# SSM layer of a decoder trunk: a group's convolution in seven steps, decay rows loaded on ScalarE's queue, and a new order of the blocks

## The chip, the core and the metric

The kernel runs on one core of a Trainium2 chip. Its time is the device time of one execution in microseconds (us); the median of three runs is given where several were made. Engines: PE (TensorE, matmuls), DVE (VectorE), ACT (ScalarE), POOL (GpSimd) and SP (SyncE, which issues transfers).

## The reference

A trunk of two layers on 256 tokens of width 2048: an attention mixer (MLA) and a state-space mixer (SSM, Mamba-2), each followed by a squared-ReLU MLP. The change touches only the SSM mixer:

```python
def ssm_mixer(h, w_in, conv_w, conv_b, dt_bias, a_log, d_skip, norm_g, w_out):
    z, xbc, dt = jnp.split(h @ w_in, [SSM_D_INNER, SSM_D_INNER + SSM_CONV_DIM], axis=-1)
    xbc = jax.nn.silu(causal_depthwise_conv(xbc, conv_w, conv_b))        # 4 taps in time
    xs, b_in, c_in = jnp.split(xbc, ...)       # x: 8 groups of 8 heads of 64; B, C: 8 groups of 128
    dt = jax.nn.softplus(dt + dt_bias)
    y = ssd_chunked_scan(xs, dt, -jnp.exp(a_log), b_in, c_in)            # one chunk of 256
    y = (y + d_skip * xs) * jax.nn.silu(z)
    y = y * lax.rsqrt(mean(y * y over a group) + RMS_EPS) * norm_g
    return y @ w_out

# in the scan, per head: cum = cumsum(dt * a); decay = exp(cum[l] - cum[s]) for s <= l
#   y[l] = sum_s (C[l] . B[s]) * decay[l, s] * dt[s] * x[s]
```

## The kernel before

**Weights.** All weights stream from HBM in units of 128x1024 (512 KB). A unit is loaded on SP's queue into one of six `raw` buffers, ACT makes its high part `wh` (line 102), DVE its low part `wl` (line 103), with four buffers each, and PE multiplies both: a unit of an ordinary block is 12 matmuls of 512 columns (lines 339, 340, 343), a unit of the seven-product blocks six (lines 1158 to 1160; some of these units DVE makes first as sums of others, line 183). Conversion runs about three units ahead of PE.

**Ticks.** PE's instructions run in the order of the program. The other engines' orders are picked by the scheduler from what depends on what. The kernel places its small work with `later(n, fn)`: `fn` is written into the program n + 1 ticks on, where a tick ends two units of a block (`block`, or 5.4 us counted by `spend` in stage A). So a small matmul stands on PE at its tick, and everything behind it waits if its operand or its PSUM bank is not there.

**PSUM.** Four banks `acc`, two `yp`, two `sm`. `bank(False)` gives an `sm` bank, `bank(True)` alternates between `yp` and `sm`. A bank is taken again when its last reader is done.

**SSM, stage A.** Block B0 (projection of B for groups 0 to 3), the narrow block dt, then two passes `ssm_seven` of seven-product blocks with other units between them (SSM_FILLERS: C0 and x4, then x5 and x6; a filler accumulates in `yp`). A B or C block is evacuated (`evac`), and `conv` takes it in two halves: transposes to an `sm` bank (line 1216), ACT and three DVE taps per piece (lines 1222 and 1225), Tanh (1227) and the product (1228). dt's narrow result is folded (line 367), a chain of some 20 small DVE steps and ACT steps makes dt and log a (lines 1255 to 1271), `cums` multiplies by a triangle to get the running sums (1277) and writes them to HBM (`cumD`), `back` transposes them (1286).

**SSM, stage B.** SSM_ORDER lists the rest: v = the convolution of a group's x (`x_conv`), x7, B1, C1, z = a group's gate projection, o = output projection. `x_conv(g)` reads rows of x back from HBM (four shifted views, four tap weights and a bias), and DVE multiplies and adds over several ticks. With it goes `cb_group(g)` (lines 1302, 1303: the product of B and C into an `sm` bank, masked by DVE, copied by ACT at 1311). Then `ahead` puts eight heads on a queue and `across` computes the far half (line 1389). In each tick `pump` takes one or two heads: `head` loads the head's row of `cumD` to all partitions (`cm`, four buffers, line 1414, on SP's queue), ACT makes exponentials (lines 1419, 1421), DVE multiplies by cb (1426). After eight heads: the products (1437, 1438), POOL and DVE add up, and the group is `ready`. `z_block(g)` computes the gate's SiLU; `gate` runs when the group is ready: POOL product, ACT squares (line 296), reciprocal root, DVE product, a POOL-issued copy (`words`), and `transposes` to an `sm` bank (lines 322, 324), which ACT and DVE empty (299, 300).

Of the kernel before, what the change touches and what calls it, by code (L numbers as in the profile page):

```python
# [20 lines left out]
F32 = mybir.dt.float32  # L21
# [7 lines left out]
P = 128  # L29
S = 256  # L30
# [184 lines left out]
class Trunk:  # L215
    def __init__(self, tc, ctx, d, out):
        self.tc, self.nc, self.d, self.out = tc, tc.nc, d, out
        nc = self.nc
        pool = lambda name, bufs, **kw: ctx.enter_context(tc.tile_pool(name=name, bufs=bufs, **kw))
        self.c = pool("const", 1)  # L220
        self.st = pool("stat", 24)
        self.res = pool("res", 1)
        self.xtp = pool("xt", 8)
        self.k4 = pool("k4", 8)
        self.s2 = pool("s2", 7)
        self.gb = pool("gb", 2)
# [4 lines left out]
        self.queue, self.pump = [], None  # L231
        self.nsm = 0
        self.uid = 0
# [9 lines left out]
    def tick(self):  # L243
        ready = []
# [926 lines left out]
    def ssm_body(self, sp, dp, gain, later):  # L1171
# [14 lines left out]
        xg = [None] * GROUPS  # L1186
        hq, ready, gated, batch = [], set(), set(), []
        far = [None] * GROUPS
# [19 lines left out]

        def conv(ev, ct, dst, lag):

            def half(j):
                b = self.bank(False)
                for k in range(2):
# [15 lines left out]
            self.later(lag, lambda: half(0))  # L1229
            self.later(lag + 1, lambda: half(1))  # L1230

# [7 lines left out]

        def bc_block(name, i, accs=None):  # L1240
            if accs is None:
                accs = self.block([("si", name, i, q) for q in range(4)], xT)
            t = self.ktile(self.k4, F32)
            fm[name, i] = t
            conv(evac(accs), (32 if name == "B" else 40) + 4 * i,
                 lambda j: t[:, 2 * j:2 * j + 2].rearrange("p a b -> p (a b)"), 0)

        def dt_block():
            self.narrow_block(("si", "dt", 0, 0), self.xT, dt_chain)

        def dt_chain(b):
# [23 lines left out]
            def cums():  # L1275
                b = self.bank(False)
                nc.tensor.matmul(b[:64, 0:256], la[:, 0], tri, start=True, stop=False)
# [18 lines left out]

            self.later(2, cums)

# [30 lines left out]

        def x_conv(g):  # L1330
            xt = sp2.tile([P, 2, 512], F32, tag="xtm", name=f"xtm{g}", bufs=4)
# [10 lines left out]

            def fetch():
                with behind("last_load"):
                    nc.sync.dma_start(xt, x_rows(g, 0, 2))
                    weight(3)
                    load(2)
                    weight(2)
                    load(1)
                    weight(1)  # L1350
                    load(0)

# [6 lines left out]
            def mult():  # L1359
                with behind("last_lo"):  # L1360
                    nc.vector.tensor_tensor(xt, xt, both(3), ALU.mult)
                    tapped(2)
                with behind("last_load"):
                    weight(0)
                    weight(4)

# [10 lines left out]
            def ahead():  # L1377
                xg[g] = x
                dg = self.gain_tile(d["dsk"][g])
                for i in range(8):  # L1380
                    hq.append((g, i, dg))
                heads_of = lambda v: v.rearrange("p (h f) -> p h f", h=8)
# [9 lines left out]

                self.later(1, across)

            self.later(0, fetch)
            self.later(1, lambda: cb_group(g))
            self.later(2, mult)
            self.later(3, lambda: tapped(1))
            self.later(4, total)
            self.later(5, lambda: (silu(), ahead()))  # L1400

        def pump():
            for _ in range(2 if len(hq) > HEAD_BACKLOG else 1):
                if hq:
                    g, i, dg = hq.pop(0)
                    head(g, i, dg)
                    if i == 7:
                        break

        def head(g, i, dg):  # L1410

            h = 8 * g + i
            cm = sp2.tile([P, S], F32, tag="cm", name=f"cm{h}", bufs=4)
            nc.sync.dma_start(cm, cumD[h:h + 1].to_broadcast([P, S]))
            if i % 4 == 0:
# [13 lines left out]
            heads = batch[:]  # L1429
            batch.clear()  # L1430

            def products():
# [26 lines left out]
        def z_block(g):  # L1459
            accs = self.block([("si", "z", g, q) for q in range(4)], xT)  # L1460
            ng = self.gain_tile(d["sng"][g])
            ssq = self.stat(2)
# [31 lines left out]
        out = {}  # L1494

        def filler(tok):
# [4 lines left out]
            if o == 7:  # L1501
                x_block(i, out[0]) if kind == "x" else bc_block(kind, i, out[0])
            self.spend(2.72)

        with ExitStack() as first:
# [12 lines left out]
        for step in SSM_ORDER:  # L1518
# [5 lines left out]
            elif kind == "v":  # L1524
                x_conv(i)
            elif kind == "z":
# [4 lines left out]
            else:  # L1531
# [128 lines left out]
def sequence(d):  # L1660
# [40 lines left out]
    so = lambda k, nb: add(("so", k, nb), d["so"][k, nb])  # L1701
    si("B", 0)
    add(("si", "dt", 0, 0), d["sidt"], 16, 64)
    for p in range(2):
# [102 lines left out]
```

## Time and profile before

| what | value |
|---|---|
| three runs | 2347.49 us median (2343.76 to 2348.76) |
| profiled execution | 2347.11 us, its span 2345.2 us |
| granted TensorE clock, mean | 0.988 |
| instructions on PE / DVE / ACT / POOL | 10881 matmuls / 2257 / 2036 / 323 |
| moved by DMA | 569.74 MB, mean 243 GB/s |
| SSM in the profile | about 975 to 1560 us; stage B from 1172 us |

Durations and starts come from the profiled execution alone. A row of a timeline is start, duration, engine, line, operation, output and inputs, count, and in brackets the idle time before it with what ended it. A row of the waits is engine, output, line, what it waited for, then microseconds in total, times, and the longest. Rows of a stage table give the length, then the busy time of PE, PEld (weight load), DVE, ACT and POOL with instruction counts, the granted clock, the DMA engines' share and GB/s.

### The profile page before, as it was taken

The page shows a single profiled execution, that of the slowest core. Times are in us where ns is not written, and L with a number is a line of the kernel's source. Part 1 is how long each engine was busy: PE and PEld are TensorE (multiplying, and loading weights), DVE is VectorE, ACT ScalarE, POOL GpSimd, SP SyncE. Part 2 cuts the span into 40 slices and gives each one's busy share as a digit, 9 for nine tenths or more (in the row PEclk, how much of TensorE's full clock was granted, in tenths as well). Part 3 has the DMA queues.
Part 4 walks back from the last instruction along what each step waited for, and adds up shares of the span by engine and source line. Part 5 has one row for each costly group of instructions (what it writes and reads, how often), then busy time and mean ns, then how long its engine had stood idle before and what let it go on. Part 6 is the DMA issues. An engine that isn't in the chain of part 4 may idle for free. (4 is left out here: it accounts for less than half of the span.)

```text
span 2345.2 us, 30882 instructions
## 1 busy us (share of the span) xinstructions
PE 2292.8 (98%) x10881; PEld 1895.2 (81%) x10881; DVE 1968.5 (84%) x2257; ACT 1439.3 (61%) x2036; POOL 269.1 (11%) x323
## 2 busy tenths in 40 slices
PE   9999999999999999989999898999999999999999
PEld 7888888888888888767877677788888888888887
DVE  7776798899899887977869787985888899889985
ACT  7775566666656656556656565664566666666663
POOL 1530000000000000000002133231000000000000
PEclk9999999999999999989999999999999999999999
DMA  8545688888888877658797677876687888888875
GB/s 316 167 160 167 206 251 246 267 253 266 276 246 263 273 216 250 199 160 280 249 338 252 228 255 264 291 238 205 216 260 240 275 259 251 258 269 250 263 232 165
DMA packets 177050, 569.74 MB, mean 243 GB/s; under 512 B 20192, under 2 KB 29344, under 8 KB 176896
## 3 DMA queue, kind: packets, MB, share of 16 engines
q1 hardware_dynamic: 159328, 510.83, 65.5%
q0 software_dynamic: 15040, 52.68, 11.0%
q10 hardware_dynamic: 2528, 4.27, 0.5%
q8 instruction: 85, 1.39, 0.3%
q14 instruction: 69, 0.57, 0.1%
HBM read 542.23 MB, written 6.41 MB: 234 GB/s over the span
## 5 line engine op out<-in xcount | busy, mean ns | idle before, releaser
L102 ACT ACTIVATE wh<-wraw 128x1024 fp32r<-128x1024 f32 (+1 forms) x818 | 857.3, 1053 | 535.6 <-PE acc L340 197.6
L103 DVE TENSOR_TENSOR wl<-wraw,wh 128x1024 fp32r<-128x1024 f32 (+1 forms) x818 | 989.2, 1227 | 191.4 <-ACT wh L102 182.3
L617 PE MATMUL yp<-wh,k 128*128 128x512 f32 x896 | 349.3, 390 | 0.0
L619 PE MATMUL yp<-wh,k 128*128 128x512 f32 x896 | 348.8, 389 | 0.0
L618 PE MATMUL yp<-wl,k 128*128 128x512 f32 x896 | 348.6, 389 | 0.0
L102 ACT ACTIVATE wh<-wrx 128x1024 fp32r<-128x1024 f32 x192 | 203.3, 1059 | 177.0 <-PE yp L619 99.1
L103 DVE TENSOR_TENSOR wl<-wrx,wh 128x1024 fp32r<-128x1024 f32 x192 | 233.2, 1220 | 46.3 <-ACT wh L102 45.7
L339 PE MATMUL acc<-wh,k 128*128 128x512 f32 x496 | 197.0, 397 | 0.0
L619 PEld LDWEIGHTS yp<-wh,k 128*128 128x128 f32 x896 | 168.2, 188 | 35.0
L617 PEld LDWEIGHTS yp<-wh,k 128*128 128x128 f32 x896 | 168.2, 188 | 34.9
L618 PEld LDWEIGHTS yp<-wl,k 128*128 128x128 f32 x896 | 168.2, 188 | 34.9
L340 PE MATMUL acc<-wh,k 128*128 128x512 f32 x496 | 193.9, 391 | 0.0
L339 PE MATMUL acc<-wh,xt 128*128 128x512 f32 x448 | 181.6, 405 | 0.0
L340 PE MATMUL acc<-wh,xt 128*128 128x512 f32 x448 | 178.2, 398 | 0.3 <-DVE xt L482 0.2
L617 PE MATMUL st<-wh,xt 128*128 128x512 f32 x448 | 177.7, 397 | 0.0
L619 PE MATMUL st<-wh,xt 128*128 128x512 f32 x448 | 174.9, 390 | 0.0
L618 PE MATMUL st<-wl,xt 128*128 128x512 f32 x448 | 174.7, 390 | 0.0
L618 PE MATMUL st<-wl,sN 128*128 128x512 f32 x336 | 131.6, 392 | 2.0 <-DVE wl L103 2.0
L617 PE MATMUL st<-wh,sN 128*128 128x512 f32 x336 | 133.1, 396 | 0.0
L343 PE MATMUL acc<-wl,k 128*128 128x512 f32 x496 | 132.7, 389 | 0.0
L199 POOL DMA_DIRECT2D wrx<-mi x56 | 49.0, 876 | 723.8 <-DVE wl L103 513.7
L619 PE MATMUL st<-wh,sN 128*128 128x512 f32 x336 | 131.1, 390 | 0.0
(340 smaller groups left out, 3842.2 us busy)
## 6 DMA issues: line engine op xcount, KB each, us to landing
wraw<-mi SPq DMA_DIRECT2D x256, 512.0 KB, 5.7
wraw<-mo SPq DMA_DIRECT2D x256, 512.0 KB, 5.5
wraw<-si SPq DMA_DIRECT2D x160, 512.0 KB, 5.5
wraw<-so SPq DMA_DIRECT2D x64, 512.0 KB, 5.2
wrx<-mi SPq DMA_DIRECT2D x56, 512.0 KB, 5.3
wrx<-mi POOLq DMA_DIRECT2D x56, 512.0 KB, 7.6
wraw<-wo SPq DMA_DIRECT2D x32, 512.0 KB, 3.9
tap<-xD SPq DMA_DIRECT2D x24, 512.0 KB, 6.8
```

Source lines behind the costliest of these rows:

```text
L102: self.last = nc.scalar.activation(h[:, v], raw[:, v], AF.Copy)
L103: self.last_lo = nc.vector.tensor_tensor(lo[:, v], raw[:, v], h[:, v].bitcast(F32), ALU.subtract)
L199: nc.gpsimd.dma_start(st["b11"].tile, quarter(d, 1, 0), accum_op=ALU.add)
L339: nc.tensor.matmul(accs[t][:, :n], ah, wh[:, q, :], start=first and kt + q == 0, stop=False)
L340: nc.tensor.matmul(accs[t][:, :n], al, wh[:, q, :], start=False, stop=False)
L343: nc.tensor.matmul(accs[t][:, :n], lhs(kt + q, t)[0], wl[:, q, :], start=False, stop=en and q == nk - 1)
L617: nc.tensor.matmul(b, ah, wh, start=first and q == 0, stop=False)
L618: nc.tensor.matmul(b, ah, wl, start=False, stop=False)
L619: nc.tensor.matmul(b, al, wh, start=False, stop=last and q == 1)
```

## The change

B0 and C0 are ordinary blocks, both ahead of dt; C0 leaves the fillers. Their convolution halves are two ticks apart (C0's three, starting three ticks on), B's and C's in alternating `yp` and `sm` banks except C0's. The fold of dt comes six ticks after its block instead of one, `cums` four instead of two ticks after the fold's tick, `back` two ticks further. `x_conv` starts after a given number of ticks, splits its loads over two ticks, and puts cb_group, the multiplications, the total and the SiLU into five further ticks; `across` comes one tick later. The rows `cm` are loaded on ACT's queue, up to two heads ahead, and the heads go two to a tick always. A gate starts two ticks after the last addition, its transposes a tick later; the gain tiles are loaded at their use. SSM_ORDER is new. PE has the same instructions as before.

```diff
-        def conv(ev, ct, dst, lag):
+        def conv(ev, ct, dst, lag, gap, wide):
 
             def half(j):
-                b = self.bank(False)
+                b = self.bank(wide)
...
             self.later(lag, lambda: half(0))
-            self.later(lag + 1, lambda: half(1))
+            self.later(lag + gap, lambda: half(1))
...
-        def bc_block(name, i, accs=None):
+        def bc_block(name, i, lag=1, gap=2, wide=True):
...
-            self.narrow_block(("si", "dt", 0, 0), self.xT, dt_chain)
+            self.narrow_block(("si", "dt", 0, 0), self.xT, dt_chain, 6)
...
-                self.later(0, back)
+                self.later(2, back)
...
-            self.later(2, cums)
+            self.later(4, cums)
...
-        def x_conv(g):
+        def x_conv(g, wait):
...
-                self.later(1, across)
-
-            self.later(0, fetch)
-            self.later(1, lambda: cb_group(g))
-            self.later(2, mult)
-            self.later(3, lambda: tapped(1))
-            self.later(4, total)
-            self.later(5, lambda: (silu(), ahead()))
+                self.later(2, across)
+
+            self.later(wait, lambda: fetch(whole, lambda: weight(3), lambda: load(2), lambda: weight(2), lambda: load(1)))
+            self.later(wait + 1, lambda: fetch(lambda: weight(1), lambda: load(0)))
+            self.later(wait + 2, lambda: cb_group(g))
+            self.later(wait + 3, mult)
+            self.later(wait + 4, lambda: tapped(1))
+            self.later(wait + 5, total)
+            self.later(wait + 6, lambda: (silu(), ahead()))
 
         def pump():
-            for _ in range(2 if len(hq) > HEAD_BACKLOG else 1):
-                if hq:
-                    g, i, dg = hq.pop(0)
-                    head(g, i, dg)
+            for _ in range(2):
+                if cms:
+                    g, i, cm = cms.pop(0)
+                    head(g, i, cm)
                     if i == 7:
                         break
-
-        def head(g, i, dg):
+            while hq and len(cms) < 2:
+                g, i = hq.pop(0)
+                cm = sp2.tile([P, S], F32, tag="cm", name=f"cm{8 * g + i}", bufs=4)
+                nc.scalar.dma_start(cm, cumD[8 * g + i:8 * g + i + 1].to_broadcast([P, S]))
+                cms.append((g, i, cm))
+
+        def head(g, i, cm):
 
             h = 8 * g + i
-            cm = sp2.tile([P, S], F32, tag="cm", name=f"cm{h}", bufs=4)
-            nc.sync.dma_start(cm, cumD[h:h + 1].to_broadcast([P, S]))
...
-                    ready.add(g)
+                    ready[g] = self.ticks + 2
...
-                if g not in ready:
+                if self.ticks < ready.get(g, self.ticks + 1):
                     self.later(0, gate)
                     return
+                ng = self.gain_tile(d["sng"][g])
...
-                    self.later(2, lambda t=t, w=w: self.transposes(w, yT[g][0], yT[g][1], t, False))
-                self.later(2, lambda: gated.add(g))
+                    self.later(3, lambda t=t, w=w: self.transposes(w, yT[g][0], yT[g][1], t, False))
+                self.later(3, lambda: gated.add(g))
...
             bc_block("B", 0)
+            bc_block("C", 0, 3, 3, False)
             dt_block()
...
-                x_conv(i)
+                x_conv(i, int(step[3:] or 0))
...
-SSM_FILLERS = [[("C", 0), ("x", 4)], [("x", 5), ("x", 6)]]
-SSM_ORDER = ["v0", "x7", "B1", "v1", "z0", "v2", "z1", "C1", "v3", "z2", "z3", "v4", "o0a", "v5", "o0b", "z4", "v6",
-             "o1a", "v7", "o1b", "z5", "z6", "o2a", "z7", "o2b", "o3"]
+SSM_FILLERS = [[("x", 4)], [("x", 5), ("x", 6)]]
+SSM_ORDER = ["v0", "x7", "v1+2", "B1", "C1", "v2", "z0", "v3+2", "z1", "z2", "v4", "z3", "v5+4", "o0a", "o0b", "v6+2", "z4",
+             "o1a", "v7", "o1b", "z5", "z6", "z7", "o2a", "o2b", "o3"]
```

Three places show what moves. In these rows `sm_739` or `wh432` are single buffers (the last number is the program's own), and brackets name the engines or DMA lanes that the instruction waits for.

PE in stage A, before: the second half of a convolution (line 1216), the fold of dt (367) and the first matmuls of a seven-product block. 24 block matmuls stand between the first half (`sm_734`) and this one, and 72 between the fold and the running sums (1277).

```order
L343 MATMUL yp_738_9105<-wl431_9028,xt_664_8481 128x512
L1216 MATMUL sm_739_9141<-ident_97,s2_730_9044 128x128 [waits DVE_49]
L1216 MATMUL sm_739_9141<-ident_97,s2_731_9046 128x128
...
L367 MATMUL sm_742_9158<-cst_96,s2_733_9085 128x64 [waits DVE_49,PE_49,Activation_49]
...
L1158 MATMUL st_744_9188<-wh432_9048,xt_664_8481 128x512
L1159 MATMUL st_744_9188<-wh432_9048,xt_665_8482 128x512
```

The same place after; the half before it is `sm_751`.

```order
L1160 MATMUL st_749_9340<-wl455_9497,sN5_719_8906 128x512
L1216 MATMUL sm_755_9552<-ident_97,s2_741_9227 128x128 [waits PE_49]
L1216 MATMUL sm_755_9552<-ident_97,s2_742_9229 128x128
...
L367 MATMUL sm_758_9569<-cst_96,s2_744_9270 128x64 [waits DVE_49,PE_49,Activation_49]
...
L1158 MATMUL st_750_9369<-wh456_9509,sN6_724_8955 128x512
L1159 MATMUL st_750_9369<-wh456_9509,sN6_725_8956 128x512
```

The half now waits for no DVE work on its bank, 72 block matmuls stand between the halves, and 120 between the fold and the running sums.

PE in stage B, before: the transposes of gate 0 (lines 322 and 324), a tile for each half of the tokens (`sm_836`, `sm_837`), with ordinary block matmuls around them.

```order
L343 MATMUL acc_833_11446<-wl553_11450,xt_677_8587 128x512
L322 MATMUL sm_836_11535<-ident_97,tr_823_11366 128x128 [waits DMASW6_49,PE_49]
L322 MATMUL sm_836_11535<-ident_97,tr_823_11366 128x128 x3
L322 MATMUL sm_837_11542<-ident_97,tr_824_11369 128x128 [waits DMASW7_49,PE_49]
L322 MATMUL sm_837_11542<-ident_97,tr_824_11369 128x128 x2
L324 MATMUL sm_837_11542<-ident_97,s2_810_11148 128x128 [waits DVE_49]
L339 MATMUL acc_832_11445<-wh554_11467,xt_690_8693 128x512 [waits Activation_49]
```

After, the same two tiles are `sm_846` and `sm_847`; `sm_845` is the product of B and C for group 3 (lines 1301 and 1302 there, 1302 and 1303 before).

```order
L343 MATMUL acc_844_11725<-wl559_11665,xt_664_8481 128x512
L1301 MATMUL sm_845_11762<-k4_740_9226,k4_729_9039 128x256 [waits PE_49]
L1302 MATMUL sm_845_11762<-k4_740_9226,k4_729_9039 128x128
L322 MATMUL sm_846_11768<-ident_97,tr_834_11515 128x128 [waits DMASW6_49]
L322 MATMUL sm_846_11768<-ident_97,tr_834_11515 128x128 x3
L322 MATMUL sm_847_11775<-ident_97,tr_835_11518 128x128 [waits DMASW7_49,DVE_49]
L322 MATMUL sm_847_11775<-ident_97,tr_835_11518 128x128 x2
L324 MATMUL sm_847_11775<-ident_97,s2_823_11454 128x128
```

Three tiles of two `sm` banks now stand in one tick, and the last of them waits for DVE's reading of an earlier one.

ACT in stage B, before: the heads 19 and 20 (both of group 2) (lines 1419 and 1421) between conversions (102) and a piece of a convolution (1222); their rows come from SP's queue.

```order
L1419 ACTIVATE mt16_11601<-cm19_11695,pcum_8830 128x128 x2
L1421 ACTIVATE mt16_11601<-mt16_11601,lndt_8832 128x128 x2
L102 ACTIVATE wh562_11731<-wraw562_11612 128x1024
L102 ACTIVATE wh563_11786<-wraw563_11630 128x1024
L1222 ACTIVATE s2_845_11752<-sm_844_11747,cst_96 128x256
L102 ACTIVATE wh564_11804<-wraw564_11711 128x1024
L1419 ACTIVATE mt20_11779<-cm20_11777,pcum_8830 128x128 x2
```

After, around the same head 20 (lines 1417 and 1419 there), with the row loads (1407) on ACT itself and the emptying of gate 0's transposes (299):

```order
L102 ACTIVATE wh562_11746<-wraw562_11662 128x1024
L1419 ACTIVATE mt16_11702<-mt16_11702,lndt_8832 128x128
L1407 DMA cm20_11794<-cumD_8833 128x256
L1407 DMA cm21_11796<-cumD_8833 128x256
L1407 DMA cm22_11855<-cumD_8833 128x256
L102 ACTIVATE wh563_11800<-wraw563_11680 128x1024
L1417 ACTIVATE mt20_11846<-cm20_11794,pcum_8830 128x128 x2
L1419 ACTIVATE mt20_11846<-mt20_11846,lndt_8832 128x128 x2
L299 ACTIVATE k4_824_11457<-sm_846_11768 128x4x128
```

The rows of heads 20 to 22 are asked for together, one conversion ahead of the first use, and the emptying of `sm_846` stands behind that use.

More of the change, by code (lines that the diff above doesn't have):

```diff
@@ L230, in __init__ @@
         self.yp = pool("yp", 2, space=PSUM)
-        self.queue, self.pump = [], None
+        self.queue, self.pump, self.ticks = [], None, 0
         self.nsm = 0
@@ L243, in tick @@
     def tick(self):
-        ready = []
+        self.ticks += 1
         for e in self.queue:
@@ L1186, in ssm_body @@
         xg = [None] * GROUPS
-        hq, ready, gated, batch = [], set(), set(), []
+        hq, cms, ready, gated, batch = [], [], {}, set(), []
         far = [None] * GROUPS
@@ L1238, in evac @@
             return ev
-        def bc_block(name, i, accs=None):
-            if accs is None:
-                accs = self.block([("si", name, i, q) for q in range(4)], xT)
+        def bc_block(name, i, lag=1, gap=2, wide=True):
+            accs = self.block([("si", name, i, q) for q in range(4)], xT)
             t = self.ktile(self.k4, F32)
@@ L1245, in bc_block @@
             conv(evac(accs), (32 if name == "B" else 40) + 4 * i,
-                 lambda j: t[:, 2 * j:2 * j + 2].rearrange("p a b -> p (a b)"), 0)
+                 lambda j: t[:, 2 * j:2 * j + 2].rearrange("p a b -> p (a b)"), lag, gap, wide)
         def dt_block():
-            self.narrow_block(("si", "dt", 0, 0), self.xT, dt_chain)
+            self.narrow_block(("si", "dt", 0, 0), self.xT, dt_chain, 6)
         def dt_chain(b):
@@ L1341, in load, with fetch, whole @@
                 nc.sync.dma_start(tap[k], x_rows(g, 0, 2, k))
-            def fetch():
+            def fetch(*todo):
                 with behind("last_load"):
[L1345 to L1351, printed above, removed]
+                    for fn in todo:
+                        fn()
+            def whole():
+                nc.sync.dma_start(xt, x_rows(g, 0, 2))
             both = lambda k: cw[k].unsqueeze(1).to_broadcast([P, 2, 512])
@@ L1362, in mult @@
                     tapped(2)
-                with behind("last_load"):
-                    weight(0)
-                    weight(4)
+                fetch(lambda: weight(0), lambda: weight(4))
             def total():
@@ L1501, in filler @@
             if o == 7:
-                x_block(i, out[0]) if kind == "x" else bc_block(kind, i, out[0])
+                x_block(i, out[0])
             self.spend(2.72)
@@ L1702, in sequence @@
     si("B", 0)
+    si("C", 0)
     add(("si", "dt", 0, 0), d["sidt"], 16, 64)
```

5 lines of the change are left out of this document (2 added, 3 removed).

## The prediction

> **What bounds the kernel now.** I read the page first (busy shares), then PE's busy time and granted clock by stage, then the waits of PE from 900 us on, and last the timelines at those waits. The page:
>
> ```profile
> span 2345.2 us, 30882 instructions
> PE 2292.8 (98%) x10881; PEld 1895.2 (81%) x10881; DVE 1968.5 (84%) x2257; ACT 1439.3 (61%) x2036; POOL 269.1 (11%) x323
> ```
>
> PE is the bound, 52 us of the span are not PE, and the change removes no matmul. So the question is which of PE's idle time goes. Lines are those of the kernel before. By stage (the end of MLP 1, SSM projections with B0, C0, dt and the seven-unit blocks = stage A, the ordered part of SSM = stage B, MLP 2):
>
> ```profile
> 940.00:975.00 35.00, 35.00 (x180) 29.74 (x180) 33.00 (x40) 20.77 (x28) 3.37 (x7) 1.00 0.75 246
> 975.00:1172.00 197.00, 180.20 (x761) 146.18 (x760) 156.76 (x177) 113.87 (x127) 7.07 (x8) 0.94 0.71 219
> 1172.00:1560.00 388.00, 360.99 (x1937) 293.47 (x1936) 319.49 (x353) 237.83 (x460) 95.98 (x62) 0.96 0.79 269
> 1560.00:1660.00 100.00, 100.00 (x516) 82.95 (x515) 66.75 (x73) 47.05 (x58) 14.31 (x14) 1.00 0.70 218
> ```
>
> The columns after the length are PE, PEld, DVE, ACT, POOL busy, then the granted clock. PE is idle 197.0 - 180.2 = 16.8 us in A and 388.0 - 361.0 = 27.0 in B, 43.8 together, and never in the stages beside them; only there is the clock below 1.00. Who ends those waits:
>
> ```profile
> PE sm L1302 <- DVE s L1225: 10.5, 2, 6.0
> PE sm L322 <- DMA tr<-s: 6.6, 4, 4.0
> PE sm L1277 <- DVE dt L1270: 6.3, 1, 6.3
> PE sm L367 <- DVE s L1225: 4.4, 1, 4.4
> PE sm L1216 <- DVE s L1225: 4.3, 1, 4.3
> PE sm L1389 <- POOL s L1385: 3.9, 1, 3.9
> PE acc L343 <- DVE wl L103: 3.1, 2, 2.0
> PE sm L322 <- ACT cb L1311: 2.9, 1, 2.9
> PE yp L339 <- ACT s L1321: 1.5, 2, 1.0
> PE sm L1216 <- ACT s L1236: 0.2, 1, 0.2
> ```
>
> In A: 6.3 + 4.4 + 4.3 + 1.5 + 0.2 = 16.7. In B: 10.5 + 6.6 + 3.9 + 3.1 + 2.9 = 27.0. Nearly all are the small matmuls (lines 322 to 1389) that wait for a chain, or for one of the two `sm` banks, at the place in PE's order where their tick puts them. What such a wait costs is more than its length:
>
> ```profile
> 1232.45 1.19 PE L1302 MATMUL sm<-k,k 128*128 128x256 f32 x2 [5.96 <-DVE s L1225]
> ...
> 1284.45 0.50 PE L322 MATMUL sm<-ident,tr 128*128 128x128 f32 x4 [1.25 <-DMA tr<-s]
> 1286.19 0.59 PE L322 MATMUL sm<-ident,tr 128*128 128x128 f32 x3 [1.24 <-DMA tr<-s]
> ...
> 1287.67 0.63 PE L339 MATMUL acc<-wh,xt 128*128 128x512 f32 x1
> 1288.09 0.63 PE L340 MATMUL acc<-wh,xt 128*128 128x512 f32 x1
> ...
> 1429.76 1.19 PE L343 MATMUL acc<-wl,xt 128*128 128x512 f32 x4 [2.01 <-DVE wl L103]
> ...
> 1432.21 0.40 PE L339 MATMUL acc<-wh,xt 128*128 128x512 f32 x1
> 1432.44 0.39 PE L340 MATMUL acc<-wh,xt 128*128 128x512 f32 x1
> ```
>
> ```profile
> 1226.49:1232.45 5.96, 0.00 (x1) 0.03 (x1) 5.63 (x8) 0.62 (x2) 0.00 (x0) 0.86 1.03 407
> 1232.45:1238.00 5.55, 5.55 (x15) 4.48 (x16) 3.39 (x7) 1.51 (x3) 0.00 (x0) 0.53 0.67 207
> ```
>
> Right after the two gaps of 1.25 and 1.24 us matmuls start 0.42 us apart; after the gap of 2.01 they start 0.23 apart, the full pace (24 of them, one tick, are 5.5 us). The stage rows give the price in sum: (1 - 0.94) x 197 = 11.8 us and (1 - 0.96) x 388 = 15.5, together 27.3, if all of the slow clock fell on matmuls. Some falls into the gaps, where it costs nothing: by the last two rows, the gap of 5.96 us and what follows it, 0.14 x 5.96 = 0.8 inside and 0.47 x 5.55 = 2.6 behind. By that share (0.76) the clock costs 20.7 us, 0.47 for each us of idle time. A microsecond of idle time removed is then worth 1.47 us (1.62 if none falls into the gaps), and all that can be had is 43.8 x 1.47 = 64 us.
>
> On this the Trainium skill ("TensorE: Matmul & The Clock Gate", section "HAM oscillation — how this bites in real kernels") says that gaps over about 3.4 us bring the half clock. The pair of 1.25 and 1.24 us disagrees. By that rule the short waits that I leave below (8.9 us) would cost no clock, and the time would come out 0.47 x 8.9 = 4 us lower than mine.
>
> **Stage A, part by part.** B0's and C0's projections go ahead of dt's, their convolution halves come two and three ticks apart, the fold of dt six ticks after its block, and the running sums (line 1277) 120 block matmuls behind the fold where they were 72. 120 x 0.227 = 27.2 us; the chain took 72 x 0.227 + 6.3 = 22.6, so the 6.3 goes with 4.6 to spare. The fold and the second half no longer follow a half 24 matmuls earlier that still holds an `sm` bank (72 now): 4.4 and 4.3 go, and 0.2. With C0 no longer a filler in `yp`, 1.5 goes too. What is late next is DVE, whose order after C0's second half now reads six taps (line 1225), two makings of a sum of weights (line 183), the product (line 1228), dt's first steps with the reciprocal, and only then the low part of unit 460:
>
> ```profile
> L103 DVE TENSOR_TENSOR wl<-wraw,wh 128x1024 fp32r<-128x1024 f32 x66 | 79.7, 1221 | 18.4 <-ACT wh L102 17.4 <-PE st L1159 0.7
> ...
> L1225 DVE SCALAR_TENSOR_TENSOR s<-sm,cst,s 128x255 f32<-128x255 f32 (+2 forms) x24 | 11.4, 476 | 0.3
> L183 DVE TENSOR_TENSOR wraw<-wraw,wraw 128x1024 f32<-128x1024 f32 x8 | 9.8, 1223 | 4.5 <-DMA wraw<-si 4.5
> ...
> L1228 DVE SCALAR_TENSOR_TENSOR k<-s,s 128x512 f32<-128x512 f32 x4 | 2.7, 687 | 0.0
> ...
> L1260 DVE RECIPROCAL dt<-dt 128x128 f32<-128x128 f32 x1 | 0.9, 943 | 0.0
> ```
>
> 6 x 0.48 + 2 x 1.22 + 0.69 + 0.94 + five small steps that I put at 0.3 (half of a tap's size, half to two thirds of its time) + 1.22 for the unit itself = 9.7, and, as an estimate, three taps' time (1.4) for the turns through ACT: 11.1 us, while PE has 32 matmuls (7.3 us) to do before it needs that unit. 3.8 are lost there, and I add 2 for the six units behind it, each with some of dt's small steps in front. **A keeps 6 us of idle time** (0 if the converted units in store cover it, 14 if a second burst follows).
>
> **Stage B.** The product of a group's B and C (line 1302) leaves the tick of a convolution half and comes two ticks after the loads: the 10.5 goes. The gate's transposes get four ticks instead of three from the gate, 5.5 us more against a longest wait of 4.0: the 6.6 goes. The far product (line 1389) gets one more tick against 3.9: it goes. The 2.9 was a transpose that wanted the bank of a cb tile; that comes back in another shape. In the tick of gate 0's transposes the order now has cb of group 3 in one `sm` bank, and both transposes have to share the other: the second waits until ACT (line 299) and DVE (line 300) have emptied the first. On ACT there stands ahead of that emptying a head of group 2, the first use of a row asked for one unit earlier. Such rows were:
>
> ```profile
> L1419 ACT ACTIVATE mt<-cm,pcum x128: 384/387/405, 1203.6 to 1543.1; 128x128 f32<-128x128 f32 x128
> L1414 SPq DMA_DIRECT2D cm<-cumD x64: 319/422/1513, 1196.3 to 1534.9; - x64
> ...
>   DMA cm<-cumD: 37.8, 17
> ...
> DMA to landing us min/median/max: 3.0/5.4/9.0
> ```
>
> ```profile
> L299 ACT ACTIVATE k<-sm 128x512 fp32r<-128x512 f32 x12 | 6.6, 586 | 4.8 <-PE sm L322 4.7
> ```
>
> ```profile
> L300 DVE TENSOR_TENSOR k<-sm,k 128x512 fp32r<-128x512 f32 x12 | 7.9, 683 | 0.3 <-ACT k L299 0.3
> ```
>
> The wait is 0.59 + 0.68 = 1.3 us if ACT stands ready, and 1.3 + 5.4 + a head's 1.2 = 7.9 if ACT has just issued the loads; I take the middle, 4.6. The same three tiles meet once more, at gate 1 with cb of group 4: again 4.6 (1.3 to 7.9). The far product of group 1 takes the bank of cb 2, whose last reader on ACT also stands behind a load: 1.8 (0 to 4.4). In group 0 the rows are asked for just ahead of each use, and the units converted behind them come late: 2 (0 to 8). The 3.1 for `wl` stays (0 to 8), since DVE's work is the same. **B keeps 4.6 + 4.6 + 1.8 + 2 + 3.1 = 16.1 us.**
>
> The moved loads themselves: 64 issues leave SP (0.42 us each there, 27 us that delay no weight as far as the waits show) and stand on ACT. With the heads two to a tick, ACT's share of a group is six ticks, 32.7 us. Its pace:
>
> ```profile
> 1203.56 0.70 ACT L1419 ACTIVATE mt<-cm,pcum 128x128 f32<-128x128 f32 x2 [2.04 <-DMA cm<-cumD]
> ...
> 1204.74 0.68 ACT L1419 ACTIVATE mt<-cm,pcum 128x128 f32<-128x128 f32 x2
> ...
> 1220.18 2.00 ACT L102 ACTIVATE wh<-wraw 128x1024 fp32r<-128x1024 f32 x2
> ```
>
> 12 conversions at 0.96, 8 heads at 1.18 and 8 issues at 0.42 are 24.3; of ACT's other work in B (237.8, less 115 conversions at 1.05 and 64 heads at 1.38 by their busy times, is 29) 3.6 falls to a group: 27.9, which leaves 4.8 us. There are four buffers of rows. The first four heads' rows are asked for well ahead; the fifth's goes out one conversion before its use, so ACT stands 5.4 - 1.0 = 4.4 us once per group: just within the 4.8, and no more than before (37.8 / 8 = 4.7 per group). So the move is taken at nothing beyond the terms above. The convolution's loads, weights and products are the same instructions in other ticks, on SP and DVE; SP ends none of PE's waits above, and the DVE work that moves is the cover that rival 2 takes away. The gain tiles, loaded a tick or more before use either way, are taken at nothing too; a late one would hold the gate's last step, which has the four ticks as cover.
>
> The Trainium skill ("DMA: Bandwidth & Descriptors", section "Issuing engines are not separate DMA queues") says that all issuers' transfers share the same 16 DMA engines and that another issuer saves issue time alone. By it the landing stays near 5.4, as taken. Were ACT's queue free of the weights in front, with the shortest landing of 3.0, each of the three waits above that stand behind a row would lose up to 2.4 us, some 11 us with the clock. No run shown so far decides it.
>
> **Sum.** Idle time left 6 + 16.1 = 22.1; gone 43.8 - 22.1 = 21.7; by 1.47 that is 31.9 us. The profiled execution took 2347.1 (span 2345.2 and 1.9 around it), the median of the runs is 2347.5, so the two serve alike: 2347.1 - 31.9 = 2315.2, or **2315**.
>
> **Rivals.**
> 1. *The waits are covered.* Converted units and ACT's slack swallow the new bank waits; some 5 us stay: 38.8 x 1.47 = 57, that is 2290. For it: each new wait has an end near zero. Against: two transposes share one bank by the order itself. Chance 0.16.
> 2. *DVE is next.* DVE is busy 157 of 197 us in A and 319 of 388 in B, and B would end nearer 360; the waits named go, but PE waits for `wl` in their place. If 37 of the 43.8 us stay, 6.8 x 1.47 = 10 us are gained: 2337. For it: the burst found in A. Against: only 3.1 us of the waits were for `wl`. Chance 0.14.
> 3. *The asking ahead is not ahead, and ACT becomes the bound (slower).* If not one but three and more of the four later rows of a group are exposed one after the other, ACT stands 13.2 us and more against 4.8 of slack: 8.4 x 8 = 67 us, about all that could be had, so three is the point from which the kernel gets slower. At 3.5 it is (15.4 - 4.8) x 8 = 85 us on a floor of 2347.1 - 64 = 2283: 2368. For it: ACT works in order, so that every conversion behind a row waits with it. Against: the four rows go out in two or three issues that stand together, and land together. Chance 0.10.
>
> **How the numbers follow.** My forecast has 0.60: 2315, by its own ends 2290 to 2340. About 0.2% (4.7 us) is what a measurement of this kernel can tell from no change. The range from 2288 to 2343 leaves out rival 3, half of rival 1 and a corner of rival 2, 0.2 together. Faster: 0.60 + 0.16 + 0.09 of rival 2 = 0.85; same 0.05; slower 0.10.
>
> **What would show it.** Right: in the waits of PE lines 1302, 1277, 367 and 1389 for DVE and POOL are gone or under 1 us; what stands there is line 322 and the block lines waiting for DVE or ACT, some 22 us in sum; the clock reads 0.97 or 0.98 in both stages; ACT's wait for the rows is 30 to 45 us. Wrong: PE waits for `wl` or `wh` by more than 15 us (rival 2), ACT's wait for the rows is above 100 us (rival 3), idle time in SSM under 8 us (rival 1), or the granted clock stays at 0.95 while the idle time falls, which would break the factor of 1.47.

## The result, and the profile after

The changed kernel takes 2331.91 us (median, 2330.64 to 2335.67) against 2347.51 for the kernel before in the same session: the ratio is 0.9939, 95% interval 0.9922 to 0.9956. It is faster by 15.6 us, half of the 32 that were forecast. Its profiled execution took 2331.0 us.

The page, then the two stages of SSM. The border between them is the first matmul of block x7, at 1169.39 us before and 1153.29 after, and stage B ends 16.0 us before the old end. First before:

```profile
975.00:1169.39 194.39, 177.59 (x749) 144.01 (x748) 155.09 (x176) 111.88 (x124) 7.07 (x8) 0.94 0.71 218
1169.39:1560.00 390.61, 363.60 (x1948) 295.64 (x1947) 321.17 (x355) 239.82 (x463) 95.98 (x62) 0.96 0.80 269
```

and after:

```profile
span 2329.2 us, 30832 instructions
PE 2281.0 (98%) x10881; PEld 1886.9 (81%) x10881; DVE 1971.9 (85%) x2257; ACT 1437.2 (62%) x2036; POOL 254.7 (11%) x323
```

```profile
975.00:1153.29 178.29, 169.79 (x762) 139.28 (x761) 153.50 (x177) 110.04 (x124) 7.07 (x8) 0.97 0.77 236
1153.29:1544.00 390.71, 358.35 (x1997) 290.84 (x1996) 320.87 (x352) 237.28 (x462) 82.22 (x62) 0.97 0.80 269
```

Stage A is 194.39 - 178.29 = 16.1 us shorter, which is the whole difference. Stage B is as long as it was. PE stands idle in it for 390.7 - 358.4 = 32.3 us where it was 27.0, and its busy time fell by as much as that grew (363.6 to 358.4), which goes with the clock of 0.97 for 0.96. The waits of PE after, in SSM (engine, output, line, what ended the wait; total, times, longest):

```profile
PE y L1437 <- DVE s L1225: 10.0, 1, 10.0
PE sm L322 <- DVE k L300: 9.5, 1, 9.5
PE sm L367 <- DVE s L1225: 8.1, 1, 8.1
PE acc L339 <- ACT wh L102: 4.7, 4, 1.7
PE acc L343 <- DVE wl L103: 4.5, 3, 2.9
PE sm L1301 <- DVE k L300: 3.0, 1, 3.0
PE sm L1216 <- ACT cb L1310: 0.6, 1, 0.6
PE st L1160 <- DVE wl L103: 0.4, 2, 0.2
```

The waits that the change was to end are gone: line 1302 (10.5), the gate's transposes for their copy (6.6), the far product (3.9), the running sums (6.3). New ones of the same size stand in stage B, three of them for a PSUM bank. The first, from PE's timeline:

```profile
1225.21 0.60 PE L1216 MATMUL yp<-ident,s 128*128 128x128 f32 x4
1231.21 0.34 PE L1437 MATMUL y<-xtm,mt 128*64 128x64 f32 x4
1241.50 3.34 PE L1437 MATMUL y<-xtm,mt 128*64 128x64 f32 x60 [9.96 <-DVE s L1225]
```

B1's second convolution half went into a `yp` bank at 1225.2, and group 0's products need both `yp` banks 6 us later. DVE gives the bank back only when the six taps of that half are done, and it was that late:

```profile
1234.54 0.48 DVE L1225 SCALAR_TENSOR_TENSOR s<-yp,cst,s 128x255 f32<-128x255 f32 x1
...
1239.85 1.50 DVE L1225 SCALAR_TENSOR_TENSOR s<-yp,cst,s 128x255 f32<-128x255 f32 x3
```

The second is the wait that the prediction named, the two transposes of gate 0 that share one `sm` bank. ACT (first fence) emptied its part 2.8 us after PE's start at 1293.75, DVE (second fence) only at 1303.0, behind all this:

```profile
1296.00 0.57 ACT L299 ACTIVATE k<-sm 128x512 fp32r<-128x512 f32 x1
```

```profile
1296.58 0.68 DVE L1424 TENSOR_TENSOR mt<-mt,cb 128x512 f32<-128x512 f32 x1
1297.18 1.21 DVE L103 TENSOR_TENSOR wl<-wraw,wh 128x1024 fp32r<-128x1024 f32 x1
1298.32 1.27 DVE L1449 SCALAR_TENSOR_TENSOR xtm<-xtm,y 128x512 f32<-128x512 f32 x2
1299.52 1.37 DVE L1424 TENSOR_TENSOR mt<-mt,cb 128x512 f32<-128x512 f32 x1
1300.81 0.48 DVE L1305 SCALAR_TENSOR_TENSOR cb<-sm,tri 128x128 f32<-128x128 f32 x2
1301.21 1.89 DVE L103 TENSOR_TENSOR wl<-wraw,wh 128x1024 fp32r<-128x1024 f32 x1
1303.02 0.68 DVE L300 TENSOR_TENSOR k<-sm,k 128x512 fp32r<-128x512 f32 x1
```

### The profile page after: what moved, and what is told of

Read it like the earlier page. It is cut to its first block, busy times and chain, and to the rows that moved or that the text cites. A ratio compares the mean times of both kernels' runs of the same rounds, so it can differ in the third digit from the quotient of the medians.

```text
span 2329.2 us, 30832 instructions
## 1 busy us (share of the span) xinstructions
PE 2281.0 (98%) x10881; PEld 1886.9 (81%) x10881; DVE 1971.9 (85%) x2257; ACT 1437.2 (62%) x2036; POOL 254.7 (11%) x323
## 4 chain that ended last, share of the span: by engine, by line
PE 88%; DVE 5%; DMA 4%; ACT 2%; issue 1%; POOL 0%; SPq 0%; ACTq 0%; DVEq 0%
PE yp L619 9%; PE yp L618 9%; PE yp L617 9%; PE acc L339 8%; PE acc L343 8%; PE acc L340 8%; PE st L618 7%; PE st L619 7%; PE st L617 7%; DMA cm<-cumD 2%; DVE wl L103 2%; PE st L1160 1%; PE st L1158 1%; PE st L1159 1%; PE yp L339 1%
## 5 line engine op out<-in xcount | busy, mean ns | idle before, releaser
L102 ACT ACTIVATE wh<-wraw 128x1024 fp32r<-128x1024 f32 (+1 forms) x818 | 856.1, 1052 | 522.4 <-PE acc L340 183.9
L103 DVE TENSOR_TENSOR wl<-wraw,wh 128x1024 fp32r<-128x1024 f32 (+1 forms) x818 | 999.3, 1240 | 197.9 <-ACT wh L102 186.4
L102 ACT ACTIVATE wh<-wrx 128x1024 fp32r<-128x1024 f32 x192 | 203.3, 1059 | 169.8 <-PE yp L619 102.9
L103 DVE TENSOR_TENSOR wl<-wrx,wh 128x1024 fp32r<-128x1024 f32 x192 | 233.7, 1222 | 40.7 <-ACT wh L102 40.2
L339 PE MATMUL acc<-wh,xt 128*128 128x512 f32 x480 | 193.0, 402 | 2.7 <-ACT wh L102 1.7
L340 PE MATMUL acc<-wh,xt 128*128 128x512 f32 x480 | 188.9, 394 | 0.0
L343 PE MATMUL acc<-wl,xt 128*128 128x512 f32 x480 | 129.4, 392 | 0.1
```

What stands on the lines that cost most here:

```text
L102: self.last = nc.scalar.activation(h[:, v], raw[:, v], AF.Copy)
L103: self.last_lo = nc.vector.tensor_tensor(lo[:, v], raw[:, v], h[:, v].bitcast(F32), ALU.subtract)
L339: nc.tensor.matmul(accs[t][:, :n], ah, wh[:, q, :], start=first and kt + q == 0, stop=False)
L340: nc.tensor.matmul(accs[t][:, :n], al, wh[:, q, :], start=False, stop=False)
L343: nc.tensor.matmul(accs[t][:, :n], lhs(kt + q, t)[0], wl[:, q, :], start=False, stop=en and q == nk - 1)
```

## The experiments

All times are medians of four runs or more; each ratio is to the kernel before, timed beside it. The changed kernel (2331.91, ratio 0.9939) was timed in a session of its own, so a difference to it in microseconds can be off by one or two: by the two ratios the 22.5 us of e5_sp below are 21.6 and the 15.3 of e12_ahead 14.1.

**Which stage gave the gain.** Two kernels, each with one stage's part.

> The kernel before with stage A's part alone: B0 and C0 as blocks ahead of dt with their new spacing, the fold six ticks on, the running sums and the step behind them later; the ordered stage B as before. Theory 1 (all of the gain comes from stage A; in stage B each wait removed was replaced by a bank wait of the same size): 16 us under before, 2331, waits in stage B as before (27 us). Rival (the two stages lean on each other, the new stage B gives some and the new stage A some): 2336 to 2342.

The main edits to the kernel before (lines are left out at the dots):

```diff
...
+            bc_block("B", 0, 1, 2, True)
+            bc_block("C", 0, 3, 3, False)
...
+            self.narrow_block(("si", "dt", 0, 0), self.xT, dt_chain, 6)
...
+                self.later(2, back)
...
+            self.later(4, cums)
...
+SSM_FILLERS = [[("x", 4)], [("x", 5), ("x", 6)]]
...
```

Measured: 2333.11, ratio 0.9947 (0.9935 to 0.9960), 12.2 us under the kernel before.

> The changed kernel with stage A's part undone: C0 a filler again, old lags there; all of the new stage B. Theory 1: no gain, 2345 to 2350, with stage A's 16.8 us of idle time back and some 32 us of idle time in stage B. Rival (stage B by itself gives what was forecast for it): 2332.

The main edits to the changed kernel (the old places of the fold, of `cums` and of `back` are among the lines left out):

```diff
...
-            bc_block("B", 0)
-            bc_block("C", 0, 3, 3, False)
+            bc_block("B", 0, 0, 1, False)
...
-SSM_FILLERS = [[("x", 4)], [("x", 5), ("x", 6)]]
+SSM_FILLERS = [[("C", 0), ("x", 4)], [("x", 5), ("x", 6)]]
...
```

Measured: 2346.87, ratio 1.0004 (0.9995 to 1.0013). Theory 1 held: the gain is stage A's (12 us of the whole change's 16, with intervals that overlap), and the new stage B by itself is worth nothing that can be measured.

**Are the new waits worth their length?** Three kernels take one each away.

> The changed kernel with both halves of B1's and C1's convolution in sm banks, so that no half holds a yp bank ahead of group 0's products. Theory 1 (the 10.0 us wait of the products is one for a bank): it goes, with the half clock behind it 10 to 14 us, 2318 to 2322, unless the halves then wait for each other in sm. Rival (DVE is full there, and PE would wait for DVE's next product anyway, as low parts of weights): at most 3 us, 2329 to 2333.

```diff
-                bc_block(kind, i)
+                bc_block(kind, i, 1, 2, False)
```

Measured: 2330.72, ratio 0.9942 (0.9929 to 0.9954), no more than 1 us under the changed kernel: the rival. The products' wait of 10.0 is gone, and in its place stand these of e3_sm's waits of PE (in the changed kernel 4.5, none and 3.0; so most of what came is a wait for ACT, which the rival did not name):

```profile
PE acc L343 <- DVE wl L103: 5.9, 6, 2.9
PE sm L1216 <- ACT s L1236: 5.1, 1, 5.1
PE sm L1301 <- DVE k L300: 4.2, 1, 4.2
```

> The changed kernel with groups 3 and 4 one tick later (v3+3, v4+1), so that cb of these groups stands a tick behind the transposes of gates 0 and 1 and not in their tick. Theory 1: the waits of 9.5 and 3.0 us for DVE's emptying (line 300) go, 2317 to 2322. Rival (DVE's queue is the limit, and what stood behind the 9.5 us comes late in another place): at most 3 us, 2329 to 2333.

```diff
-... "v3+2", "z1", "z2", "v4", ...
+... "v3+3", "z1", "z2", "v4+1", ...
```

Measured: 2318.66, ratio 0.9882 (0.9867 to 0.9897), 13 us under the changed kernel: theory 1. The 9.5 of line 322 is 0.5 here; line 1301, now one tick behind the transposes, waits 7.1 in two for the same emptying.

> The kernel of e4_cb with the product of B and C of groups 3 to 6 one tick later still, two behind the gate's transposes. Theory 1: its two waits of 3.5 us for DVE's emptying go, 2311 to 2316. Rival (DVE's queue is the limit): 2317 to 2321, the 7 us in other waits for DVE.

The edit to e4_cb:

```diff
-self.later(wait + 2, lambda: cb_group(g))
+self.later(wait + (3 if g in (3, 4, 5, 6) else 2), lambda: cb_group(g))
```

Measured: 2319.87, ratio 0.9896 (0.9879 to 0.9913): no gain over e4_cb. Line 1301's waits went, and the far product (line 1383) now waits 4.2 for line 300 and the block line 339 3.6 for line 299. That is the rival.

**The fold of dt in stage A.** It stands directly behind C0's second half. From PE's timeline of the changed kernel, and DVE's:

```profile
1038.79 1.09 PE L367 MATMUL sm<-cst,s 128*128 128x64 f32 x4 [8.12 <-DVE s L1225]
```

```profile
1037.12 1.52 DVE L1225 SCALAR_TENSOR_TENSOR s<-sm,cst,s 128x255 f32<-128x255 f32 x3 [0.63 <-ACT s L1222]
```

The last three taps of that half end at 1038.64, and the fold starts 0.15 us later. Which bank or operand ties it to these taps the profile does not say.

> The kernel of e4_cb with dt's fold (line 367) eight instead of six ticks after its block, 48 block matmuls (10.9 us) behind C0's second half instead of directly behind it. Theory 1 (the fold waits for the last tap of the half directly ahead, 8.1 us): the wait goes, with its half clock 8 to 12 us, 2307 to 2311. Rival (DVE is full there, and PE would wait for low parts of weights instead): 2316 to 2321, waits of lines 1160 and 343 grown by 5 us or more.

The edit to e4_cb:

```diff
-self.narrow_block(("si", "dt", 0, 0), self.xT, dt_chain, 6)
+self.narrow_block(("si", "dt", 0, 0), self.xT, dt_chain, 8)
```

Measured: 2310.38, ratio 0.9853 (0.9834 to 0.9872), 8.3 us under e4_cb; line 367 is gone from the waits, and those for low parts in stage A grew by 1.2. Theory 1 held.

**The row loads.** They were moved from SP's queue to ACT's.

> The changed kernel with its row loads (cm) issued on SP's queue at the same places instead of ACT's. Theory 1 (the queue of these loads ends no wait of PE): 2329 to 2334, as the changed kernel. Rival (loads on ACT hold up its conversions, or stay clear of the weights in SP's queue): 4 us or more to either side, with PE's waits for high parts of weights (4.7 us) gone or grown.

```diff
-nc.scalar.dma_start(cm, cumD[8 * g + i:8 * g + i + 1].to_broadcast([P, S]))
+nc.sync.dma_start(cm, cumD[8 * g + i:8 * g + i + 1].to_broadcast([P, S]))
```

Measured: 2309.40, ratio 0.9847 (0.9829 to 0.9865). One word of the kernel is worth 22.5 us, more than the whole change. Theory 1 fell here. The tile's view, changed kernel first, then e5_sp:

```profile
L1407 ACTq DMA_DIRECT2D cm<-cumD x64: 326/350/578, 1150.5 to 1524.9; - x64
...
  DMA cm<-cumD: 28.0, 14
...
DMA to landing us min/median/max: 3.0/5.3/8.0
```

```profile
L1407 SPq DMA_DIRECT2D cm<-cumD x64: 319/422/1260, 1180.1 to 1494.0; - x64
...
  DMA cm<-cumD: 13.4, 8
...
DMA to landing us min/median/max: 3.0/4.9/9.3
```

The landing is about the same. What differs is when the issue comes: on ACT it stands in line between the conversions, and in the changed kernel the first head starts at 1163.2 us, in e5_sp at 1187.0. ACT's timeline in group 0 of the changed kernel shows an issue that holds ACT up behind an older load (3.17), and two landings waited for:

```profile
1161.82 0.33 ACTq L1407 DMA_DIRECT2D cm<-cumD  x1
1162.25 1.06 ACT L102 ACTIVATE wh<-wraw 128x1024 fp32r<-128x1024 f32 x1 [3.17 <-DMA xtm<-xD]
...
1168.02 0.70 ACT L1417 ACTIVATE mt<-cm,pcum 128x128 f32<-128x128 f32 x2 [3.53 <-DMA cm<-cumD]
...
1176.07 0.70 ACT L1417 ACTIVATE mt<-cm,pcum 128x128 f32<-128x128 f32 x2 [4.87 <-DMA cm<-cumD]
```

Each holds up the conversions behind it, and DVE with them. How long DVE's low parts waited for ACT's high parts in stage B stands behind the last bar, at "ACT wh L102"; the changed kernel first, then e5_sp (25.4 in the kernel before):

```profile
L103 DVE TENSOR_TENSOR wl<-wraw,wh 128x1024 fp32r<-128x1024 f32 x115 | 156.9, 1378 | 44.6 <-ACT wh L102 41.9 <-PE acc L343 2.6
```

```profile
L103 DVE TENSOR_TENSOR wl<-wraw,wh 128x1024 fp32r<-128x1024 f32 x116 | 149.1, 1297 | 24.4 <-ACT wh L102 21.9 <-ACT mt L1417 2.3
```

PE's waits for `wh` (4.7) are gone in e5_sp, `wl` falls from 4.5 to 0.5, the products from 10.0 to 5.1, line 322 from 9.5 to 6.9: stage B keeps 14.6 us of idle time.

Theory 2, from here on: ACT, through which every unit of weights goes, loses its lead when it stands at the rows. Three kernels ask in what way.

> The changed kernel with up to four rows asked for ahead instead of two, still on ACT's queue and with four buffers. Theory 2, if the landing is what ACT stands for: its wait for the rows falls from 28 us to under 15, and the time to 2312 to 2322. If it is the issue itself (an issue waits for an older transfer, and all conversions behind it wait too): the wait for the rows falls, but the time stays at 2327 to 2334.

```diff
-            while hq and len(cms) < 2:
+            while hq and len(cms) < 4:
```

Measured: 2316.62, ratio 0.9879 (0.9865 to 0.9893), 15.3 us under the changed kernel, still on ACT's queue; ACT's wait for the rows is 2.6 us. So two thirds of the price go with the landing that ACT stands for; were it the issue alone, the time would have stayed. The first head starts as early as before (1164.2 against 1163.2), so these two thirds do not come from heads that start later, as they do in e5_sp.

> The changed kernel with its row loads issued on GpSimd's queue. Theory 2 (the loads cost 22 us on ACT because ACT, which converts every unit of weights, stands still at their issue and at their landing): off ACT they cost little, 2307 to 2316. Rival (what helped in e5_sp is the place in SP's queue behind the weights, so that the heads come later): near the changed kernel, 2326 to 2334.

```diff
-nc.scalar.dma_start(cm, cumD[8 * g + i:8 * g + i + 1].to_broadcast([P, S]))
+nc.gpsimd.dma_start(cm, cumD[8 * g + i:8 * g + i + 1].to_broadcast([P, S]))
```

Measured: 2326.46, ratio 0.9924 (0.9909 to 0.9939): 5 us under the changed kernel, 17 above e5_sp: inside the rival's range, near its lower end, and 10 us above theory 2's. The rival's reason cannot be most of it, since e12_ahead gained its 15.3 us with heads as early as here. ACT's wait for the rows is still 16.2, and POOL now stands 90.0 us for free row buffers (38.0 put down to line 1417, 52.0 to line 1419) with the gates' and groups' products behind it; PE's wait in line 322 is 10.5. To be off ACT is not enough. That the loads need an issuer with nothing urgent behind them is argued from this, not tried.

> e12_ahead (rows asked for up to four ahead, on ACT's queue) with the rows of group 0 alone on SP's queue. What is open: e12_ahead keeps 7 us more than e5_sp. Theory 2a (they are in group 0, where ACT's first issues stand 3.2 us behind a load of x and its heads come 23 us earlier): 2308 to 2312. Theory 2b (they are spread, some tenths of a us at each of ACT's 64 issues): 2314 to 2318.

The edit to e12_ahead:

```diff
-nc.scalar.dma_start(cm, ...)
+(nc.sync if g == 0 else nc.scalar).dma_start(cm, ...)
```

Measured: 2315.02, ratio 0.9872 (0.9858 to 0.9885), 1.6 us under e12_ahead, inside its spread. So most of the 7 us is not in group 0; 2b is what is left of the two, but it was not measured by itself, and the scheduler also orders ACT and DVE otherwise in each of these kernels. Where exactly they go stays open.

**Together.**

> e10_cb2 and e7_fold together, and B1's and C1's halves in sm banks as in e3_sm. Theory 1: the gains of the parts add up, e3_sm's being 1: 2302 to 2308. Rival (each freed wait is taken up by the next one for DVE): 2310 or more.

(e10_cb2, e7_fold and e3_sm; rows still on ACT.) Measured: 2309.26, ratio 0.9849 (0.9831 to 0.9866), 1 us from e7_fold: nearer the rival.

> e5_sp, e4_cb and e7_fold together: row loads on SP's queue, groups 3 and 4 a tick later, the fold two ticks later. Theory 2 (the gains are of separate waits): 8.3 us and 6.9 us of PE's waits in e5_sp go, with their half clock 18 to 22 us: 2287 to 2293. Rival (each freed wait is taken up by DVE's next product): 2300 to 2308.

(e4_cb, e7_fold and e5_sp.) Measured: 2294.84, ratio 0.9792 (0.9777 to 0.9808). 14.6 us under e5_sp, between the two expectations, nearer theory 2. These are all of its waits of PE from the start of SSM on:

```profile
PE sm L1301 <- DVE k L300: 4.8, 3, 2.2
PE y L1437 <- DVE s L1225: 4.7, 1, 4.7
PE st L1160 <- DVE wl L103: 2.0, 4, 1.2
```

> e13_best and also the product of B and C of groups 3 to 6 another tick later and B1's and C1's halves in sm banks. Theory 2: the 5.1 us in which group 0's products wait and the 2.1 us of line 1301 go as well: 2281 to 2287. Rival (as e3_sm and e10_cb2 showed on the changed kernel, these two move the waits on): within 3 us of e13_best.

(e8_all with e5_sp.) Measured: 2292.37, ratio 0.9778 (0.9764 to 0.9792): the rival here too, 2.5 us, but the fastest kernel of the study, 53 us under the kernel before and 40 under the changed one.

> e13_best with rows asked for up to four ahead on SP's queue. Theory 2 (ACT's wait for the rows, 9.5 us there, ends no wait of PE any more): 2292 to 2297, as e13_best. Rival (a wait of ACT for rows still costs PE as much as it lasts): 2283 to 2289.

(e13_best with the edit of e12_ahead.) Measured: 2295.33, ratio 0.9788 (0.9775 to 0.9802), as e13_best, the time of theory 2. But the edit did not take away what it was to take away: ACT waits 11.8 us for the rows here and 9.5 in e13_best. So the run shows only that on SP's queue asking for four ahead brings nothing. That the 9.5 us cost PE nothing is supported by e13_best's list alone, where no wait of PE is for ACT.

## Why the prediction was wrong

The direction and the range held; the size did not: 15.6 us for 32. Stage B was forecast at (27.0 - 16.1) x 1.47 = 16.0 us and gave nothing. Of the signs that I had named for being wrong none came (PE waits 9.6 us for `wl` and `wh`, ACT 28.0 for the rows, the idle time in SSM is 40.9, the clock 0.97), so they could not have told; of those for being right, line 367 still waits 8.1 us, and the idle time is 40.9 where I had 22.

**Stage A** was forecast at (16.8 - 6) x 1.47 = 15.9 us and gave 16.1, by errors that cancel. The waits of line 1277 (6.3), of the convolution half (4.3) and of `yp` (1.5) went as reasoned. The step "The fold and the second half no longer follow a half 24 matmuls earlier that still holds an `sm` bank" was wrong for the fold: its 4.4 became 8.1, and it starts as the taps of the half directly ahead of it end; moved away from that half, it does not wait (e7_fold). The burst at unit 460 that I priced at 3.8 + 2 cost 0.4. In part that is because PE stood at the fold while DVE worked, but in e7_fold, where it does not stand there, it is 2.0. So 8.3 us of idle time went, not 10.8, and each was worth 1.94 us, not 1.47.

**The price of idle time.** By the stage rows the clock costs (1 - 0.97) x 391 = 11.7 us in the new stage B with 32.3 us of idle time, against 15.6 with 27.0; the clock has two digits there, so each may be off by 2 us. Two gaps, of 10.0 and 9.5 us, hold most of the idle time now, and long gaps cost less for each microsecond. The rows of the changed kernel: the gap of 9.96 us and what follows it, the gap of 9.47 and what follows it, then what follows the gaps of 3.02 and 2.85, in which the clock was 1.00.

```profile
1231.54:1241.50 9.96, 0.01 (x1) 0.03 (x1) 9.74 (x13) 3.82 (x6) 1.04 (x1) 0.64 1.02 372
1241.50:1247.00 5.50, 5.50 (x70) 5.05 (x71) 1.92 (x2) 5.43 (x16) 2.14 (x2) 0.72 0.67 261
1294.28:1303.75 9.47, 0.00 (x1) 0.00 (x1) 9.47 (x13) 3.74 (x11) 3.04 (x3) 0.76 0.96 325
1303.75:1310.00 6.25, 6.25 (x19) 5.04 (x20) 2.37 (x5) 3.53 (x9) 0.71 (x1) 0.55 0.79 273
1346.45:1352.00 5.55, 5.55 (x18) 4.55 (x19) 3.44 (x7) 2.40 (x7) 0.49 (x1) 0.69 0.78 252
1459.34:1465.00 5.66, 5.66 (x18) 4.49 (x19) 5.66 (x6) 1.06 (x1) 0.00 (x0) 0.70 0.74 216
```

One less the clock, times the length, is what the half clock takes: 1.5, 2.8, 1.7 and 1.7 us behind the four gaps. The two long gaps cost 4.3 us of clock together and the two of 3 us 3.4, because much of their half clock, 3.6 and 2.3 us by the same product, fell into the gap itself. The factor is no constant of the kernel.

**Stage B**, the moved loads. This step failed: "the move is taken at nothing beyond the terms above". It cost 22.5 us (e5_sp). I compared sums, 4.4 us of standing in 4.8 us of slack for a group, and ACT's wait for rows against the 37.8 before; that wait did come out lower, 28.0, far from the 100 us that I had named as the sign of trouble. What I had not priced is what stands behind the stall: DVE waits for high parts 41.9 us where it waited 25.4, and the waits for banks that DVE gives back are longer (10.0 and 9.5 us where e5_sp has 5.1 and 6.9). That two thirds of the price go with the landings is shown (e12_ahead). That stalls of 3 to 5 us in a row use up the lead of the converted units is argued from the timeline, not tried by itself. A long stall alone does not do it. The kernel before had this one, and DVE did not wait for a high part at all between 1400 and 1450 us:

```profile
1417.10 0.69 ACT L1419 ACTIVATE mt<-cm,pcum 128x128 f32<-128x128 f32 x2 [5.47 <-DMA cm<-cumD]
```

In group 0 of the changed kernel five stalls (3.17, 3.53, 4.87, 0.98 and 3.26 us) fall within 31 us, and DVE waits 18.1 us for high parts between 1150 and 1200 us, against 8.5 in e5_sp. But the way over DVE is argued too: from 1150 to 1550 us its waits for high parts are 33.1 us in e16_g0, which takes 2315, and 28.9 in e11_pool, which takes 2326, so this sum alone does not order the kernels. Rival 3 had this mechanism and its price as too large, 2368, because it let PE wait for all of it. Without the move the forecast for stage B would have been near: 14.6 us of idle time in e5_sp against 16.1 forecast, and 2309 against 2315 in all. That is partly luck, since the parts differ: 6.9, 5.1, 2.1 and 0.5 measured, of which the 5.1 (the products) was not in my sum.

**Stage B**, the banks. The three removed waits were right. The bank shared by gate 0's transposes was right as to place (9.5 measured, 4.6 taken, 7.9 the upper end), and wrong as to reason: ACT was done 2.8 us after the first transposes began, and then 6.5 us passed in DVE's own order ahead of its step of 0.68, which was all that I had counted. The same at gate 1 was 3.0 for 4.6. I did not see the 10.0 of the products: the convolution halves that left `sm` for `yp` hold what group 0 needs; I had read that edit only as relief for `sm`.

**The clock.** The Trainium skill ("TensorE: Matmul & The Clock Gate", section "HAM oscillation — how this bites in real kernels") names gaps over about 3.4 us. In the changed kernel the gaps of 3.02 us (at 1346.45) and 2.85 us (at 1459.34) were followed by 512-column matmuls of 0.63 us in place of 0.39, those of 1.66 (1432.49) and 1.35 us (1440.30) were not. So gaps under 3 us can bring the half clock here, and the two of them that by that rule cost no clock cost 1.7 us each (rows above). Nor does the length of one gap decide alone: in the kernel before the pair of 1.25 and 1.24 us brought it, the single gap of 2.01 did not.

## What to carry to other kernels

Price a moved transfer by what stands behind its issue and its first use on the new engine, not by the engine's free time in sum: an in-order engine that every tile passes through is the wrong issuer unless the transfer has landed long before. When small work is spread over ticks, list for every tick which tiles hold which PSUM banks and how long the emptying engine's own queue is in front of the release. And undo each part of a change by itself: here one gave 16 us, one gave 22 us back, and what was left of the gain looked like one modest success.

## What the runs showed of the hardware

DVE's low parts can be slow while POOL computes: two that take 1.22 us each took 6.03 together (3.79 and 2.32), while POOL ran three products. Of the 1010 low parts in this trace, the 956 beside which POOL computed nothing took at most 1.23 us. The 3.6 us that DVE lost here stand shortly ahead of the wait of 9.5 us for its emptying at 1303; how much of that wait they are was not tried. From the changed kernel, DVE and then POOL:

```profile
1285.18 6.03 DVE L103 TENSOR_TENSOR wl<-wraw,wh 128x1024 fp32r<-128x1024 f32 x2
```

```profile
1285.33 2.54 POOL L1441 TENSOR_TENSOR xtm<-xtm,gb 128x512 f32<-128x512 f32 x2
1287.95 2.17 POOL L1443 TENSOR_TENSOR xtm<-xtm,far 128x512 f32<-128x512 f32 x1
```
